# The last layer's gate and value columns: two of four 512-column pairs as seven block products, with weight sums made in earlier layers

## The chip, the cores and the metric

The kernel runs on one core of one Trainium2 chip. The metric is the device time of one execution in microseconds (us), the median over runs. The engines are TensorE (PE, with its weight loads PEld), VectorE (DVE), ScalarE (ACT), GpSimd (POOL), and SyncE (SP), which here only issues DMAs.

## What is computed

A decoder trunk of four residual layers on x of 256 tokens by 1024 channels, all in float32. Each layer normalises x by its rms (h) and adds a mixer's output. Layers 0 and 3 are of kind A, layer 1 is dilated attention (B), layer 2 is pooling (C). Only kind A is changed:

```python
def mixer_a(h, w_in, v_gain, w_s, b_s, w_out):
    proj = h @ w_in
    u = proj[..., :A_WIDTH]                                   # A_WIDTH = 2048
    v = rms_norm(proj[..., A_WIDTH:2 * A_WIDTH], v_gain)
    z = proj[..., 2 * A_WIDTH:]
    ...
    mixed = jnp.einsum('gij,bcjgd->bcigd', ws, v) + b_s.T[None, None, :, :, None]
    y = u * mixed * jax.nn.silu(z)
    return y @ w_out
```

So h (256 x 1024) is multiplied by three blocks of 2048 columns, v, z and u; v is mixed over tokens by lower-triangular matrices of 128 x 128 (two per 512 columns), and u, mixed v and silu(z) are multiplied and projected back.

## The kernel before

**Float32 products in three passes.** Every operand of a matmul is split into a high part (ACT, `hi_of`, L82) and a low part, the rest (DVE, `lo_of`, L85). `mm3` (L75 to L79) makes one product of three matmuls: high by high, high by low, low by high.

**Weights as a stream.** All weights lie in DRAM in the order of use, as 272 units of 128 x 1024 (512 KB). `load_units` (L131) issues each from SP into one of 4 raw buffers `wr`; a raw buffer is free when DVE has made the low part of the unit that lay there. `split_hi` and `split_units` (L141, L151) make `w..h` and `w..l` into 7 buffers, some 5 units ahead of use. PE uses a unit in 12 matmuls of 128x512 (two row blocks, two token halves, three passes). In layer 3 the units are: v 208 to 223, then for each n of 0 to 3 z and u with four units each (z0 224 to 227, u0 228 to 231, z1 232 and on), and 256 to 271 for the output projection.

**Order of the work.** The program is written out by one Python thread. Projections are loops that call `step` (L167) after each row block; it calls `tick` (L102), which advances a counter and lets tasks that are due write out their next instructions. A task is a generator that yields the number of ticks until its next piece. So the code's order, and with it each engine's queue, comes from these delays; each engine then works through its queue in that order.

**Kind A.** `layer_a` (L489) makes v for n of 0 to 3 (`v_task`, L501: square sums on ACT, times gain on DVE, split), then for each n projects z, applies silu on ACT (L593), projects u; `mix_task` (L544) makes the token mix into PSUM and `y_task` (L558) multiplies on DVE (L566, L569), transposes y on PE (L577) through the one PSUM bank `tr`, and splits it (`y..h`, `y..l`). PSUM has four banks `pp` for projections, one `tr`, three `at`. In kind A layers (`gated`, L208) x isn't normalised before it is transposed: the rms factor r of a token is applied later, in silu, in the squares of v, in u (L566), and in the mixing matrices (POOL, L527). Layers 1 and 2 scale x first into a tile `xs` (`norm_scale`, L240).

**Attention (layer 1).** For each pair of heads hp and group g a projection gives q and k; `qk_task` (L635) normalises them (ACT L654), rotates (DVE L663 to L668), transposes token half 0 on PE (L675) into `tr`, splits it (ACT L677, DVE `low`, L683, written to `qk..l`), then does the same with half 1, in the same bank.

## Time and profile before

| | us |
|---|---|
| median of 3 runs | 837.23 |
| lowest and highest run | 836.3, 837.82 |
| the profiled execution | 837.29 |
| its span, first to last instruction | 835.6 |
| PE busy | 829.3 (99%) |
| DVE busy | 543.9 (65%) |
| ACT busy | 491.6 (59%) |
| mean DMA rate over the span | 179 GB/s |

A row of the timeline is: start, duration, engine and line, operation, written tile <- read tiles, shapes, count; in brackets the idle time of that engine just ahead and what ended it. A row of a group ends in: busy us in all, mean ns of one | idle time ahead, and its releaser. The granted clock of PE was 1.000. Matmuls are pipelined: one of 128x512 is shown as 0.39 us long, but the next starts earlier, and the spacing of starts is what counts. A window row has: window, length, busy us (instructions) of PE, PEld, DVE, ACT and POOL, the granted clock, DMA share and GB/s.

### The profile page before, as it was taken

How to read it: one execution, taken by the hardware profiler on the slowest of the kernel's cores; microseconds unless marked ns; L12 is line 12 of the kernel's file. 1: busy time of each engine (PE TensorE's matmuls, PEld its weight loads, DVE VectorE, ACT ScalarE, POOL GpSimd, SP SyncE). 2: the span in 40 equal slices, each digit the busy share in tenths (PEclk: the TensorE clock that was granted, in tenths of full speed). 3: DMA queues.
4: the chain of work that ended last, by engine and by line, in shares of the span. 5: the costliest groups of instructions: out<-in, count | busy, mean ns of one | idle time of the engine just before them, and what ended most of it. 6: DMA issues, size and time to landing. Idle time of an engine off the chain costs nothing.

```text
span 835.6 us, 12346 instructions
## 1 busy us (share of the span) xinstructions
PE 829.3 (99%) x4589; PEld 718.1 (86%) x4589; DVE 543.9 (65%) x906; ACT 491.6 (59%) x913; POOL 43.6 (5%) x71
## 2 busy tenths in 40 slices
PE   8999999999999999999999999999999999999998
PEld 7888888888988888888888889999988888888886
DVE  4876656646757577577577575898754777556551
ACT  6765444436758687787787576455544666434340
POOL 1201000000000010010010021000000000000000
PEclk9999999999999999999999999999999999999999
DMA  7876565562745345345355278447564466454541
GB/s 285 281 239 220 177 201 180 175 200 83 256 165 178 109 158 187 111 161 183 110 164 181 62 225 279 161 136 257 197 225 152 141 233 209 157 184 160 176 151 51
DMA packets 42028, 149.58 MB, mean 179 GB/s; under 512 B 4880, under 2 KB 5408, under 8 KB 41840
## 3 DMA queue, kind: packets, MB, share of 16 engines
q1 hardware_dynamic: 40704, 144.72, 52.1%
q0 software_dynamic: 976, 3.79, 1.3%
q8 instruction: 36, 0.59, 0.3%
q10 hardware_dynamic: 288, 0.28, 0.1%
q14 instruction: 24, 0.20, 0.1%
HBM read 147.72 MB, written 1.05 MB: 178 GB/s over the span
## 4 chain that ended last, share of the span: by engine, by line
PE 99%; DMA 1%; SPq 0%; DVE 0%; issue 0%
PE wo L77 6%; PE wo L79 6%; PE wo L78 6%; PE qk L77 5%; PE qk L79 5%; PE qk L78 5%; PE v L77 5%; PE v L79 5%; PE v L78 5%; PE z L79 4%; PE z L77 3%; PE z L78 3%; PE u L77 3%; PE u L78 3%; PE u L79 3%; PE cz L77 2%
## 5 line engine op out<-in xcount | busy, mean ns | idle before, releaser
L650 POOL TENSOR_TENSOR qr<-qm,m 128x8 f32<-128x8 f32 x12 | 19.7, 1638 | 227.9 <-DVE qm L649 227.9
L645 ACT ACTIVATE junk<-qk 128x128 bf16<-128x128 f32 x96 | 26.7, 278 | 7.3 <-PE qk L79 4.7
L566 DVE SCALAR_TENSOR_TENSOR sz<-u,m,sz 128x512 f32<-128x512 f32 x16 | 11.9, 746 | 27.3 <-PE u L79 27.3
L654 ACT ACTIVATE qn<-qk,qr 128x128 f32<-128x128 f32 x96 | 27.6, 382 | 3.4 <-POOL qr L650 3.4
L459 DVE TENSOR_TENSOR x<-wo,x 128x512 f32<-128x512 f32 x16 | 11.0, 690 | 20.1 <-PE wo L79 20.0
L255 ACT ACTIVATE hT<-hp,gT 128x128 fp32r<-128x128 f32 x48 | 13.1, 383 | 14.9 <-PE hp L251 14.9
L649 DVE TENSOR_SCALAR qm<-qs 128x8 f32<-128x8 f32 x12 | 2.1, 172 | 26.8 <-ACT junk L645 26.8
L260 DVE SCALAR_TENSOR_TENSOR hT<-hp,gT,hT 128x128 fp32r<-128x128 f32 x48 | 13.5, 343 | 8.8 <-ACT hT L255 8.8
L593 ACT ACTIVATE sz<-z,m 128x512 f32<-128x512 f32 x16 | 10.7, 687 | 13.9 <-PE z L79 13.9
L645 ACT ACTIVATION_READ_ACCUMULATOR junk<-qk 128x1 f32 x96 | 18.8, 196 | 0.0
L506 ACT ACTIVATE junk<-v,m 128x512 bf16<-128x512 f32 x16 | 11.0, 686 | 11.6 <-PE v L79 11.4
L507 DVE TENSOR_TENSOR vv<-v,kc 128x512 f32<-128x512 f32 x16 | 10.7, 687 | 8.8 <-ACT junk L506 8.4
L229 ACT ACTIVATE junk<-x 128x512 bf16<-128x512 f32 x16 | 10.2, 640 | 9.6 <-DVE x L459 9.4
L744 ACT ACTIVATE p<-p,rl 128x384 f32<-128x384 f32 (+1 forms) x16 | 11.5, 769 | 4.8 <-DVE rl L743 4.8
L569 DVE SCALAR_TENSOR_TENSOR yy<-mx,bs,sz 128x256 f32<-128x256 f32 x32 | 14.0, 479 | 0.6
L675 PE MATMUL qt<-ident,qn 128*128 128x128 f32 x96 | 14.4, 272 | 0.0
L667 DVE TENSOR_TENSOR rb<-qn,kcb 128x32 f32<-128x32 f32 x96 | 13.8, 185 | 0.0
L675 PEld LDWEIGHTS qt<-ident,qn 128*128 128x128 f32 x96 | 11.7, 140 | 2.3
L237 POOL TENSOR_TENSOR r<-ms,m 128x1 f32<-128x1 f32 x4 | 3.1, 785 | 175.3 <-DVE ms L234 175.3
L740 ACT ACTIVATE p<-p,nb 128x768 f32<-128x768 f32 x8 | 7.5, 937 | 7.6 <-DVE nb L739 7.6
L663 DVE TENSOR_TENSOR ra<-qn,kcb 128x64 f32<-128x64 f32 x48 | 10.6, 221 | 1.0 <-ACT qn L654 0.4
L775 PE MATMUL pt<-ident,p 128*128 128x128 f32 x48 | 9.9, 274 | 0.0
(2771 smaller groups left out, 3254.4 us busy)
## 6 DMA issues: line engine op xcount, KB each, us to landing
wr<-in_wts_dram SPq DMA_DIRECT2D x271, 512.0 KB, 3.9
kc<-in_a_wsT_dram POOLq DMA_DIRECT2D x2, 512.0 KB, 7.5
kc<-in_a_v_gain_dram POOLq DMA_DIRECT2D x1, 1024.0 KB, 5.1
out_dram<-x SPq DMA_DIRECT2D x4, 256.0 KB, 2.0
kc<-in_a_v_gain_dram POOLq DMA_DIRECT2D x1, 768.0 KB, 6.6
kcb<-in_masks_dram POOLq DMA_DIRECT2D x1, 576.0 KB, 8.2
x<-in_x_dram SPq DMA_DIRECT2D x2, 256.0 KB, 4.2
x<-in_x_dram SPq DMA_DIRECT2D x1, 512.0 KB, 6.6
```

The costliest lines, as they stand in the source:

```text
L77: nc.tensor.matmul(out_ap, lh[0], rh[0], start=start, stop=False, skip_group_check=True)
L78: nc.tensor.matmul(out_ap, lh[0], rh[1], start=False, stop=False, skip_group_check=True)
L79: nc.tensor.matmul(out_ap, lh[1], rh[0], start=False, stop=stop, skip_group_check=True)
L255: nc.scalar.activation(h_parts(layer)[0][:, k, t * P:(t + 1) * P], pt[:, k % 4], AF.Copy, scale=gT[:, layer, k:k + 1])
L260: nc.vector.scalar_tensor_tensor(hTl, pt[:, k % 4], gT[:, layer, k:k + 1], hTh.bitcast(F32), op0=ALU.mult, op1=ALU.subtract)
L566: nc.vector.scalar_tensor_tensor(us[t], up[t], r_tok[t][:, 0:1], us[t], op0=ALU.mult, op1=ALU.mult)
L569: nc.vector.scalar_tensor_tensor(y[:, sl], mxs[n][t][:, sl], bsT[:, 2 * n + gg:2 * n + gg + 1], us[t][:, sl], op0=ALU.add, op1=ALU.mult)
L645: nc.scalar.activation(junk[:, :HD], ov[t][:, h], AF.Square, accum_out=ssq[t][:, h:h + 1])
L650: nc.gpsimd.tensor_tensor(rqs, ms, m05_row[:, :8], op=ALU.pow)
L654: nc.scalar.activation(qn[t][:, h], ov[t][:, h], AF.Copy, scale=rq[t][:, h:h + 1])
L667: nc.vector.tensor_tensor(rb[:, hs, s0:s0 + 16], qn[t][:, hs, s1:s1 + 16], c, op=ALU.mult)
L675: nc.tensor.transpose(pts[t][:, h], qn[t][:, h], ident)
```

## The change

For n = 1 and n = 3 of layer 3 (`SEVEN`) the pair z, u is made by a scheme of seven block products. h is taken as two token halves by two channel halves, the weights of z and u as two channel halves by two column blocks (z and u): a 2 x 2 by 2 x 2 block product, in eight block products before. With sums of blocks of h and of weights on the one side, and additions of results on the other, seven suffice. A block product is 12 matmuls of 128x512 and uses two units of weights in six matmuls each.

- `sums_of_quarters`: four of the seven products need sums of weight blocks. They are made in 16 parts, each of four quarters of 128 x 256 that are loaded into one tile (`qs`, the buffer of `xs`; 512 KB), added by four DVE operations in place, and stored to DRAM (`sums`). Load, 6 ticks, additions, 3 ticks, store, 4 ticks, next load. Five parts begin in layer 0 after v, eleven in layer 1 after the first qk projection.
- The weight stream of a changed pair has 14 units: eight from `sums` and six of the units as before (the other two are read for the sums alone). Units after it are counted on, so that the stream has 284.
- `sums_task` makes the sums of blocks of h during v's third and fourth projection of layer 3: eight additions of 128x512 on DVE, and four splits.
- Since sums of token halves can't carry one factor r per token, layer 3 now scales x first, as layers 1 and 2 do (`late` instead of `gated`).
- `seven_products` accumulates into four `pp` banks: zb (two products), xb (three), yb and wb. ACT copies intermediate sums out: q5 from zb, p1, n2 and n3 from xb, where a later product adds to the same bank. DVE combines them (`first_task`, `second_task`) ahead of `y_task`.

Cut from the diff: the DRAM pool, a bound (`n_seq` in `split_units`), and the places in `v_task` where r is left out when not `late`.

```diff
 LAST_LAG = 1
 LAST_AHEAD = 3
 WARM = 13
+SEVEN = (1, 3)
+FIRST_PARTS = 5
 @with_exitstack
...
     loaded = [0]
     split = [0]
+    seq = list(range(n_units))
+    sums = {(n, j): dp.tile([4, P, UNIT], F32, name=f"sums{n}{j}") for n in SEVEN for j in range(2)}
+    def seven_units(n):
+        return n_units - 48 + 8 * n
+    for n in reversed(SEVEN):
+        z = seven_units(n)
+        seq[z:z + 8] = [e[j] for e in (((n, 0, 0), (n, 0, 1)), (z, z + 1), (z + 6, z + 7), ((n, 3, 0), (n, 3, 1)),
+                                       (z + 2, z + 3), ((n, 2, 0), (n, 2, 1)), ((n, 1, 0), (n, 1, 1)))
+                        for j in range(2)]
+    n_seq = len(seq)
     def load_units(n):
-        while loaded[0] < min(n, n_units):
-            u = loaded[0]
-            raw = wp.tile([P, 2, HALF], F32, tag="wr", name=f"wr{u}", bufs=RAW_BUFS)
-            nc.sync.dma_start(raw, wts[u].rearrange("p (k n) -> p k n", n=HALF))
+        while loaded[0] < min(n, n_seq):
+            i = loaded[0]
+            raw = wp.tile([P, 2, HALF], F32, tag="wr", name=f"wr{i}", bufs=RAW_BUFS)
+            src = sums[seq[i][0], seq[i][2]][seq[i][1]] if isinstance(seq[i], tuple) else wts[seq[i]]
+            nc.sync.dma_start(raw, src.rearrange("p (k n) -> p k n", n=HALF))
             raws.append(raw)
             loaded[0] += 1
+    def sums_of_quarters(parts):
+        for n, j, c in parts:
+            z = seven_units(n) + j
+            cs = slice(c * 256, (c + 1) * 256)
+            q = cp.tile([P, 4, 256], F32, tag="xs", name=f"qs{n}{j}{c}", bufs=1)
+            nc.sync.dma_start(q, wts[z:z + 8:2][:, :, cs].rearrange("i p c -> p i c"))
+            yield 6
+            for a, b in ((0, 2), (2, 3), (3, 0), (1, 3)):
+                nc.vector.tensor_tensor(q[:, a], q[:, a], q[:, b], op=ALU.add)
+            yield 3
+            nc.sync.dma_start(sums[n, j][:, :, cs].rearrange("i p c -> p i c"), q)
+            yield 4
     lowered = [0]
     def split_hi(n):
-        while split[0] < min(n, n_units):
+        while split[0] < min(n, n_seq):
             u = split[0]
             load_units(u + 1)
             hi, lo = pair(wp, [P, 2, HALF], "w", f"w{u}", W_BUFS)
...
         split_units(u + 1)
         return units[u]
-    def step(i, ahead=AHEAD):
-        tick()
+    def step(i, ahead=AHEAD, due=True):
+        if due:
+            tick()
         if i % 2 == 0:
             split_hi(used[0] + ahead)
         else:
...
     nc.gpsimd.memset(m05_row[:, :8], -0.5)
     r_rows = [m05_row[:, 8 * t + 8:8 * t + 9] for t in range(2)]
-    def gated(layer):
-        return layer in (0, DEPTH - 1)
+    def late(layer):
+        return layer == 0
     r_tok = [None, None]
     def h_parts(layer):
-        o = 16 if gated(layer) else 0
+        o = 16 if layer in (0, DEPTH - 1) else 0
         return [hT[:, o + i * KT * S:o + (i + 1) * KT * S].rearrange("p (k s) -> p k s", s=S) for i in range(2)]
     hcur = [None, None]
...
     def norm_rms(layer, t, ss):
         ms = tiny(1, f"ms{layer}{t}")
         nc.vector.scalar_tensor_tensor(ms, ss[:, 0:1], EPS, ss[:, 1:2], op0=ALU.add, op1=ALU.add)
-        r = r_rows[t] if gated(layer) else tiny(1, f"r{layer}{t}")
+        r = r_rows[t] if late(layer) else tiny(1, f"r{layer}{t}")
         r_tok[t] = r
         nc.gpsimd.tensor_tensor(r, ms, m05[:, 0:1], op=ALU.pow)
         return r
     def norm_scale(layer, t, r):
-        if gated(layer):
+        if late(layer):
             return xt[t].rearrange("p (n c) -> p n c", c=HALF)
         xs = cp.tile([P, 2, HALF], F32, tag="xs", name=f"xs{layer}{t}", bufs=1)
         for n in range(2):
...
             ys = []
             for t in range(2):
                 y = tmp("yy", f"yy{layer}{n}{t}", 2)
-                nc.vector.scalar_tensor_tensor(us[t], up[t], r_tok[t][:, 0:1], us[t], op0=ALU.mult, op1=ALU.mult)
+                if late(layer):
+                    nc.vector.scalar_tensor_tensor(us[t], up[t], r_tok[t][:, 0:1], us[t], op0=ALU.mult, op1=ALU.mult)
+                else:
+                    nc.vector.tensor_tensor(us[t], up[t], us[t], op=ALU.mult)
                 for gg in range(2):
                     sl = slice(gg * 256, (gg + 1) * 256)
                     nc.vector.scalar_tensor_tensor(y[:, sl], mxs[n][t][:, sl], bsT[:, 2 * n + gg:2 * n + gg + 1],
...
                     yield 1
             done.add(("y", layer, n))
+        if layer == DEPTH - 1:
+            smh, sml = pair(pl, [P, 4, 4, P], "sm", f"sm{layer}", 1)
+        def sums_task():
+            q = {}
+            for k, t in ((1, 1), (0, 1), (0, 0), (1, 0)):
+                d = q[k, t] = tmp("sz", f"sq{layer}{k}{t}", 4).rearrange("p (k c) -> p k c", c=P)
+                hh, hl = (a[:, 4 * k:4 * k + 4, t * P:(t + 1) * P].bitcast(F32) for a in hcur)
+                nc.vector.tensor_tensor(d, hh, hl, op=ALU.add)
+                yield 1
+            a11, a12, a21, a22 = q[0, 0], q[1, 0], q[0, 1], q[1, 1]
+            for i, (d, a, b, op) in enumerate(((a22, a21, a22, ALU.subtract), (a21, a11, a21, ALU.subtract),
+                                               (a11, a22, a11, ALU.subtract), (a12, a12, a11, ALU.add))):
+                nc.vector.tensor_tensor(d, a, b, op=op)
+                hi_of(smh[:, i], d)
+                yield 1
+                lo_of(sml[:, i], d, smh[:, i])
+                yield 1
+            done.add(("sums", layer))
+        S_A21_A22, S_A11_A21, S_REST, S_A12_REST = range(4)
+        def seven_products(n):
+            need(("sums", layer))
+            def sm(i):
+                return lambda k: (smh[:, i, k], sml[:, i, k])
+            def product(o, a, first):
+                for j in range(2):
+                    w = next_unit()
+                    for kk in range(2):
+                        k = 2 * j + kk
+                        mm3(o, a(k), (w[0][:, kk], w[1][:, kk]), first and k == 0, k == 3)
+                        step(kk, due=kk == 1)
+            def minus(o, name):
+                d = tmp("vv", name, 2)
+                nc.scalar.activation(d, o, AF.Copy, scale=-1.0)
+                return d
+            def keep(o, name):
+                d = tmp("sz", name, 4)
+                nc.scalar.activation(d, o, AF.Copy)
+                return d
+            r = {}
+            def keep_task(key, how, o):
+                r[key] = how(o, f"{key}{layer}{n}")
+                yield 1
+            zb = pp(f"zb{layer}{n}")
+            product(zb, sm(S_A21_A22), True)
+            spawn(keep_task("q5", keep, zb), 1)
+            xb = pp(f"xb{layer}{n}")
+            product(xb, lambda k: h_t(k, 0), True)
+            spawn(keep_task("p1", keep, xb), 1)
+            product(zb, sm(S_A12_REST), False)
+            product(xb, sm(S_REST), False)
+            spawn(keep_task("n2", minus, xb), 1)
+            yb = pp(f"yb{layer}{n}")
+            product(yb, lambda k: h_t(4 + k, 0), True)
+            z0, u0 = r["p1"], r["n2"]
+            def first_task():
+                nc.vector.tensor_tensor(z0, yb, z0, op=ALU.add)
+                nc.scalar.activation(z0, z0, AF.Silu)
+                yield 1
+                nc.vector.tensor_tensor(u0, zb, u0, op=ALU.add)
+            spawn(first_task(), 1)
+            spawn(mix_task(n), 2)
+            product(xb, sm(S_A11_A21), False)
+            spawn(keep_task("n3", minus, xb), 1)
+            wb = pp(f"wb{layer}{n}")
+            product(wb, lambda k: h_t(4 + k, 1), True)
+            z1, u1 = r["n3"], r["q5"]
+            def second_task():
+                nc.vector.tensor_tensor(u1, u1, z1, op=ALU.add)
+                nc.vector.tensor_tensor(z1, wb, z1, op=ALU.subtract)
+                nc.scalar.activation(z1, z1, AF.Silu)
+                yield 1
+            spawn(second_task(), 1)
+            spawn(y_task(n, (u0, u1), (z0, z1)), 2)
         for n in range(4):
             spawn(v_task(n, first if first and n == 0 else
                          proj_tok(f"v{layer}{n}", skew=layer if n == 0 else None)))
+            if layer == DEPTH - 1 and n == 0:
+                spawn(sums_task(), 4)
+        if layer == 0:
+            spawn(sums_of_quarters(parts[:FIRST_PARTS]))
         for n in range(4):
+            if layer == DEPTH - 1 and n in SEVEN:
+                seven_products(n)
+                continue
             zp = proj_tok(f"z{layer}{n}")
             us = []
             for t in range(2):
                 sz = tmp("sz", f"sz{layer}{n}{t}", 4)
-                nc.scalar.activation(sz, zp[t], AF.Silu, scale=r_tok[t][:, 0:1])
+                nc.scalar.activation(sz, zp[t], AF.Silu, scale=r_tok[t][:, 0:1] if late(layer) else 1.0)
                 us.append(sz)
             spawn(mix_task(n), 4)
             spawn(y_task(n, proj_tok(f"u{layer}{n}"), us))
...
             for g in range(NG):
                 spawn(qk_task(hp, g, proj_tok(f"qk{hp}{g}", skew=layer if hp == 0 and g == 0 else None)))
                 if hp == 0 and g == 0:
+                    spawn(sums_of_quarters(parts[FIRST_PARTS:]))
                     gate(0)
                     gate(1)
             o = proj_tok(f"v01{hp}")
...
     box = {}
+    parts = [(n, j, c) for n in SEVEN for j in range(2) for c in range(4)]
     def after_ws():
         spawn(load_b())
```

On DVE in layer 1, the second half's rotation of qk10, the split of unit 101, and the low part of qk10's first half (`qk10l`); `ra`, `rb`, `qn` are the rotation's tiles. Before:

```order
L663 TENSOR_TENSOR ra101_2839<-qn101_2749,kcb_634 128x64
L667 TENSOR_TENSOR rb101_2840<-qn101_2749,kcb_634 128x2x16 x2
L668 TENSOR_TENSOR qn101_2749<-ra101_2839,rb101_2840 128x4x32
L85 TENSOR_TENSOR w101l_2849<-wr101_2688,w101h_2848 128x1024
L683 SCALAR_TENSOR_TENSOR qk10l_2745<-qt100_2866,gv_638,qk10h_2744 128x2x128 x2
L85 TENSOR_TENSOR w102l_2874<-wr102_2742,w102h_2873 128x1024
```

and now, with the additions of one part (`qs301`: n = 3, j = 0, c = 1, of each the index in `parts`):

```order
L803 TENSOR_TENSOR ra101_2910<-qn101_2820,kcb_646 128x64
L807 TENSOR_TENSOR rb101_2911<-qn101_2820,kcb_646 128x2x16 x2
L808 TENSOR_TENSOR qn101_2820<-ra101_2910,rb101_2911 128x4x32
L170 TENSOR_TENSOR qs301_2792<-qs301_2792 128x256 x4
L88 TENSOR_TENSOR w101l_2920<-wr101_2757,w101h_2919 128x1024
L823 SCALAR_TENSOR_TENSOR qk10l_2816<-qt100_2941,gv_650,qk10h_2815 128x2x128 x2
L88 TENSOR_TENSOR w102l_2949<-wr102_2813,w102h_2948 128x1024
```

The block of four additions stands between the rotation and the split of w101, so `qk10l` stands behind it.

On DVE in layer 0, between the y products of n = 0 (`yy001`) and its low parts `y00l`; the second of the 16 parts, in the changed kernel:

```order
L612 SCALAR_TENSOR_TENSOR yy001_765<-mx001_711,bs0_254,sz001_666 128x256 x2
L88 TENSOR_TENSOR w29l_778<-wr29_687,w29h_777 128x1024
L170 TENSOR_TENSOR qs101_727<-qs101_727 128x256 x4
L88 TENSOR_TENSOR y00l_760<-yp000_786,y00h_759 128x4x128
L88 TENSOR_TENSOR w30l_807<-wr30_719,w30h_806 128x1024
L88 TENSOR_TENSOR y00l_760<-yp001_815,y00h_759 128x4x128
```

Before, the row of `qs101` is not there, and `y00l` follows w29l.

On ACT in layer 3, the highs of the weights and the first pair changed (n = 1). Before, with the two silu (`sz31`) and the highs of y (`y31h`):

```order
L593 ACTIVATE sz310_7484<-z31_0_7396,m05_66 128x512
L593 ACTIVATE sz311_7486<-z31_1_7397,m05_66 128x512
L82 ACTIVATE w241h_7496<-wr241_7420 128x1024
L82 ACTIVATE w242h_7514<-wr242_7445 128x1024
L82 ACTIVATE w243h_7546<-wr243_7464 128x1024
L82 ACTIVATE w244h_7564<-wr244_7482 128x1024
L82 ACTIVATE w245h_7594<-wr245_7506 128x1024
L82 ACTIVATE y31h_7576<-yp310_7603 128x4x128
```

and now, from the copy of p1 on:

```order
L673 ACTIVATE p131_7615<-xb31_7571 128x512
L85 ACTIVATE w242h_7623<-wr242_7569 128x1024
L85 ACTIVATE w243h_7635<-wr243_7585 128x1024
L85 ACTIVATE w244h_7647<-wr244_7603 128x1024
L85 ACTIVATE w245h_7660<-wr245_7618 128x1024
L668 ACTIVATE n231_7666<-xb31_7571 128x512
L85 ACTIVATE w246h_7674<-wr246_7630 128x1024
L85 ACTIVATE w247h_7686<-wr247_7642 128x1024
L697 ACTIVATE p131_7615<-p131_7615 128x512
```

The copy n2 of the accumulator xb stands behind the highs of four units, w242 to w245; PE's third product into xb stands behind n2.

More of the change, by code (lines that the diff above doesn't have):

```diff
@@ L505, in v_task @@
             for t in range(2):
[L506 removed]
+                nc.scalar.activation(junk, o[t], AF.Square, scale=r_tok[t][:, 0:1] if late(layer) else 1.0,
+                                     accum_out=vs[t][:, n:n + 1])
                 nc.vector.tensor_tensor(vv[t], o[t], kc[:, n * HALF:(n + 1) * HALF], op=ALU.mult)
```

12 lines of the change are left out of this document (7 added, 5 removed).

## The prediction

> **What bounds the kernel now.** I read the page's busy times and its chain first, then what TensorE (PE) waited for.
>
> ```profile
> PE 829.3 (99%) x4589; PEld 718.1 (86%) x4589; DVE 543.9 (65%) x906; ACT 491.6 (59%) x913; POOL 43.6 (5%) x71
> PE 99%; DMA 1%; SPq 0%; DVE 0%; issue 0%
> PE warm L223 <- POOL m L205: 1.4, 1, 1.4
> PE hp L327 <- DMA x<-in_x_dram: 0.7, 2, 0.4
> ```
>
> PE works for 829.3 of 835.6 us, and its only waits (2.1 us) lie at the start. So every matmul that goes is a gain of its full spacing, and every new wait of PE is a loss of its full length: nothing downstream can give it back. DVE is idle for a third of the time, but off PE's path only as long as PE's inputs and PSUM banks are ready when PE comes. The question is what 16 blocks of additions, put into DVE's queue at fixed places, and a denser stretch in layer 3 do to these margins.
>
> **What it removes.** Per changed pair, 96 matmuls of 128x512 become 84, twice: 24 go. Their spacing stands in PE's timeline in layer 3; from the first matmul of w243 to the first of w245 there are two units, 24 matmuls:
>
> ```profile
> 747.65 0.39 PE L77 MATMUL z<-w243h,hT 128*128 128x512 f32 x1
> 753.09 0.39 PE L77 MATMUL u<-w245h,hT 128*128 128x512 f32 x1
> ```
>
> 753.09 - 747.65 = 5.44 us. That is the whole gain: **-5.44**.
>
> **The sums of quarters.** Each of the 16 parts is four additions of 128x256 in a chain, the later ones reading what an earlier one wrote. Nearest rows:
>
> ```profile
> L798 DVE TENSOR_TENSOR szT<-o,szT 128x256 f32<-128x256 f32 x8 | 3.4, 422 | 4.2 <-PE o L79 4.1
> L569 DVE SCALAR_TENSOR_TENSOR yy<-mx,bs,sz 128x256 f32<-128x256 f32 x32 | 14.0, 479 | 0.6
> 299.79 0.28 DVE L667 TENSOR_TENSOR rb<-qn,kcb 128x32 f32<-128x32 f32 x2
> 300.11 0.29 DVE L668 TENSOR_TENSOR qn<-ra,rb 128x128 f32<-128x128 f32 x1
> 300.32 1.22 DVE L85 TENSOR_TENSOR w101l<-wr,w101h 128x1024 fp32r<-128x1024 f32 x1
> 301.76 0.88 DVE L683 SCALAR_TENSOR_TENSOR qk10l<-qt,gv,qk10h 128x256 fp32r<-128x256 f32 x2 [0.22 <-ACT qk10h L677]
> 303.44 0.60 PE L675 MATMUL qt<-ident,qn 128*128 128x128 f32 x4
> 303.79 0.48 PE L77 MATMUL qk<-w98h,hT 128*128 128x512 f32 x1
> ```
>
> An independent operation starts about 0.08 before the last one ends (300.11 + 0.29 against 300.32), one that needs the last result 0.04 after its end (rb's end 300.07, qn 300.11). A part thus holds DVE for 4 x 0.422 + 3 x 0.04 - 0.08 = 1.73, taken as 1.75 us; at 0.479 each and 0.1 between them it is 2.2, and without the waits (3 x 0.34 + 0.42 - 0.08) 1.36. I take 1.75, since the chain is there in the code. The Trainium skill, page "VectorE: DVE Perf Modes", section "The DRAIN you can't avoid", says that the next operation does not start before the pipe is empty and that a semaphore between two costs nothing extra. By that the chain costs what unchained additions do, the 1.36; the rows above speak against it, an overlap of 0.08 without a dependence and a gap of 0.04 with one.
>
> Where does such a block delay PE? In layer 1, PE's second group of transposes (qt) takes the one "tr" bank over from DVE's low(0), and low(0) ends just ahead: 301.76 + 0.88 = 302.64, PE at 303.44, room 0.80. The order of the changed kernel puts a block two rows ahead of low(0) there. Idle time of DVE on the way absorbs some (0.22): 1.75 - 0.22 - 0.80 = 0.73 us of wait. The same reading at the other places where a block stands ahead of a low(0) or, in layer 0, of y00l:
>
> ```profile
> 80.42 0.69 DVE L85 TENSOR_TENSOR y00l<-yp,y00h 128x512 fp32r<-128x512 f32 x1
> 82.35 0.60 PE L577 MATMUL yp<-ident,yy 128*128 128x128 f32 x4
> 215.89 1.23 DVE L85 TENSOR_TENSOR w75l<-wr,w75h 128x1024 fp32r<-128x1024 f32 x1 [0.18 <-ACT w75h L82]
> 217.30 0.87 DVE L683 SCALAR_TENSOR_TENSOR qk00l<-qt,gv,qk00h 128x256 fp32r<-128x256 f32 x2 [0.19 <-ACT qk00h L677]
> 218.98 0.60 PE L675 MATMUL qt<-ident,qn 128*128 128x128 f32 x4
> 321.76 1.23 DVE L85 TENSOR_TENSOR w108l<-wr,w108h 128x1024 fp32r<-128x1024 f32 x1 [0.19 <-ACT w108h L82]
> 325.53 0.88 DVE L683 SCALAR_TENSOR_TENSOR qk12l<-qt,gv,qk12h 128x256 fp32r<-128x256 f32 x2 [0.40 <-ACT qk12h L677]
> 327.26 0.49 PE L675 MATMUL qt<-ident,qn 128*128 128x128 f32 x3
> 388.06 0.88 DVE L683 SCALAR_TENSOR_TENSOR qk22l<-qt,gv,qk22h 128x256 fp32r<-128x256 f32 x2 [0.40 <-ACT qk22h L677]
> 389.79 0.60 PE L675 MATMUL qt<-ident,qn 128*128 128x128 f32 x4
> 434.98 1.23 DVE L85 TENSOR_TENSOR w140l<-wr,w140h 128x1024 fp32r<-128x1024 f32 x1 [0.19 <-ACT w140h L82]
> 438.74 0.88 DVE L683 SCALAR_TENSOR_TENSOR qk31l<-qt,gv,qk31h 128x256 fp32r<-128x256 f32 x2 [0.39 <-ACT qk31h L677]
> 440.43 0.60 PE L675 MATMUL qt<-ident,qn 128*128 128x128 f32 x4
> ```
>
> y00l: room 82.35 - 81.11 = 1.24, wait 0.51. qk00l: idle 0.37, room 0.81, wait 0.57. qk12l: 0.59 and 0.85, 0.31. qk22l: 0.40 and 0.85, 0.50. qk31l: 0.58 and 0.81, 0.36. With qk10l the six make **+2.98**. At 1.36 a part they make 0.8; at 2.2 a part 5.7. The other ten blocks stand ahead of weight splits alone, or of a group's second low, which nothing soon waits for; a split unit is used many us after it is made (w245l below ends at 742.41, its first matmul starts at 753.09), so I cost them at nothing. Without that lead they would be 1.75 each, 17.5 in all.
>
> The loads and stores of the parts (16 x 2 x 512 KB) go through SP, between the weight loads. A store waits there for its additions, and the next part's load waits for that store to land, both with weight loads behind them. The worst place is layer 0, where loads land late:
>
> ```profile
> wr<-in_wts_dram SPq DMA_DIRECT2D x7, 512.0 KB, 6.4
> kcb<-in_masks_dram POOLq DMA_DIRECT2D x1, 576.0 KB, 8.2
> wr<-in_wts_dram SPq DMA_DIRECT2D x271, 512.0 KB, 3.9
> ```
>
> The first two are from the window of 60 to 80 us, the last from the whole span (last column: us from issue to landing). From the store of the first part to the additions of the second there are ten ticks, each of six matmuls (1.36 us): 13.6. A store and a load at 6.4 each take 12.8 and are in time, so I take 0; at 8.2 each they take 16.4, and the additions, right ahead of y00l, come 2.8 late. That is the upper bound.
>
> **Layer 3's norm** is now scaled ahead of the transposes (4 more 128x512 operations on DVE). The same form already runs into layers 1 and 2, and its 32 transposes had 0.1 us of idle time in all:
>
> ```profile
> L251 PE MATMUL hp<-ident,xs 128*128 128x128 f32 x32 | 4.2, 273 | 0.1
> ```
>
> So **+0.1**, at most 0.5 for one late r. The eight additions, four highs and four lows for the sums of h lie under the v products, where DVE is idle for 30% (14.02 of 20 us busy); they are 8 x 0.69 there, spread over two projections, and nothing waits for them before the first changed pair:
>
> ```profile
> 700.00:720.00 20.00, 20.00 (x97) 16.80 (x96) 14.02 (x17) 9.52 (x11) 0.00 (x0) 1.00 0.54 180
> ```
>
> **The stretch of seven products.** A unit of weights is now used by six matmuls, 5.44 / 4 = 1.36 us, so a product of two units takes 2.72. The stretch has 14 units where the pair had 8. And the accumulators zb and xb are used again, so PE must wait until ACT has copied them out. Take before's stretch with T0 = 738.52 as a template:
>
> ```profile
> 736.00 1.06 ACT L82 ACTIVATE w245h<-wr 128x1024 fp32r<-128x1024 f32 x1 [3.12 <-PE u L79]
> 738.52 0.39 PE L77 MATMUL z<-w240h,hT 128*128 128x512 f32 x1
> 741.19 1.21 DVE L85 TENSOR_TENSOR w245l<-wr,w245h 128x1024 fp32r<-128x1024 f32 x1
> 742.52 0.69 DVE L85 TENSOR_TENSOR y31l<-yp,y31h 128x512 fp32r<-128x512 f32 x1
> L593 ACT ACTIVATE sz<-z,m 128x512 f32<-128x512 f32 x16 | 10.7, 687 | 13.9 <-PE z L79 13.9
> wr<-in_wts_dram SPq DMA_DIRECT2D x10, 512.0 KB, 3.3
> ```
>
> The last row is the window from 736 to 770. DVE leaves the last pair's y work at T0 + 2.67. Then by the order come five lows (1.22 less the overlap of 0.08, so 1.14 each) and two y lows up to w241l: 2.67 + 5 x 1.14 + 2 x 0.69 = 9.75, about 9.9 with one wait for ACT. Only then is w245 loaded (four raw buffers); landing 3.3 to 3.9 later gives 13.2 to 13.8; its high takes 1.06, and behind it on ACT stands n2, the copy of xb, 0.69: done at 14.9 to 15.6. PE wants xb for the sixth product after five products and two groups of transposes, 5 x 2.72 + 2 x 0.45 = 14.5 (a group of four shifts the matmuls by 0.35, 303.44 to 303.79, and 0.1 after it, an estimate from the 0.48 of the next one). Wait 0.4 to 1.1, taken as 0.8; the earlier copy p1 comes out 0.1 late at most by the same count (w241 lands at T0 + 7.1, copy done 8.85, wanted 9.06), taken as 0.1. Two stretches: **+1.8**, bounds 0.2 and 3.0 (a slow landing). Weights themselves are not late: nine units are split or loaded at T0.
>
> **Sum.** -5.44 + 2.98 + 0.1 + 1.8 = -0.56. The profiled execution took 837.29 (span 835.6 and 1.7 outside), the median of the runs is 837.23, so 837.29 - 0.56 = **836.7 us**. About 0.2% (1.7 us) is what a measurement of this kernel can tell from no change, so the likeliest answer is "the gain is eaten". With the bounds of the terms (0.8 to 5.7, 0.2 to 3.0) this case runs from 834.5 to 839.
>
> **Rivals.** *The covers hold* (0.25): the additions run closer to 1.36, DVE catches up, n2 is in time. Then -5.44 + 0.8 + 0.2 = -4.4, 832.9; with the middle term for n2, 834.5. For it: DVE is idle 35% of the time. Against: rooms of 0.8 are smaller than any block.
>
> *Slower: the raw buffers pace the stretch* (0.10). One unit passes four raw buffers in (landing + 1.06 + 1.22) / 4; at a landing of 3.9 that is 1.54, just PE's mean of 21.5 / 14, at 6.4 (the row of 60 to 80 us) 2.17. w241, the first not staged at T0, would be split at 3.9 + 6.4 + 2.3 = 12.6, in time for 13.1, but each of the next four falls 0.64 back: 2.1 us late by w245, 4.2 over both stretches, so 836.7 + 4.2 = 840.9. It decides from a landing of 5.4 on. For it: 14 units (7.34 MB) in 21.5 us are 341 GB/s, and the busiest stretches now reach 356. Against: landings in layer 3 are now near 3.3 to 3.9.
>
> ```profile
> 762.71 0.39 PE L77 MATMUL z<-w248h,hT 128*128 128x512 f32 x1
> 758.00:760.00 2.00, 2.00 (x11) 1.64 (x10) 0.33 (x1) 0.00 (x0) 0.00 (x0) 1.00 0.96 356
> ```
>
> (21.5 is the pair of before, 762.71 - 738.52 = 24.2, less 12 matmuls.) The Trainium skill, page "DMA: Bandwidth & Descriptors", section "Specifications", gives about 358 GB/s as what HBM lets one core have; the row agrees. By that limit the 14 units take 20.5 us, an estimate, so the rate alone would not make them late, only with other traffic beside it.
>
> *Slower: dearer additions* (0.08): 2.2 a part gives 5.7 in place of 2.98, 839.4; at about 1.85 (six waits 0.1 longer) nothing is left of the gain, and the loss grows from there.
>
> *Not what it says* is excluded by the order: 84 matmuls stand there for 96.
>
> **Chances.** Forecast 0.57, most of it within 1.7 of 837.2. Faster by over 0.2% (under 835.6): 0.25 and some 0.10 of the forecast, 0.35. Slower (over 838.9): 0.10 + 0.08, 0.18. Same: 0.47. The range takes in the dearer additions and most of the first rival, and leaves out the raw buffers and the first rival's best end: 833.0 to 839.6.
>
> **What would show it.** In the profile after: PE waits for DVE qk..l at five places in layer 1 and for y00l in layer 0, 0.3 to 0.7 each, 3 us in all; PE waits for ACT n2 ahead of xb's third use, 0.8 twice; four qs additions in about 1.8 us; no PE wait on w..l. Wrong: no waits on low(0) (the first rival), or waits on w..l or wr in layer 3 (the second).

## The result, and the profile after

The changed kernel took 843.58 us (median of 4 runs, 843.26 to 846.08), the kernel before 836.82 beside it (836.3 to 837.82): ratio 1.0086, interval 1.0064 to 1.0108. It is 6.8 us slower, where 0.5 less was forecast and 839.6 was the range's upper end.

The page of the profile after, its busy times and its chain:

```profile
PE 827.1 (98%) x4565; PEld 713.0 (85%) x4565; DVE 593.8 (71%) x1006; ACT 508.5 (60%) x937; POOL 42.0 (5%) x69
PE 83%; DVE 7%; DMA 5%; ACT 3%; issue 2%; POOL 0%; DVEq 0%; SPq 0%; ACTq 0%
```

The chain was PE for 99%; now 17% of it is something else. What PE waited for (us in all, times, longest):

```profile
PE xb L80 <- ACT n L668: 2.5, 2, 1.5
PE yp L620 <- DVE y00l L88: 2.5, 1, 2.5
PE yp L620 <- DVE y31l L88: 1.1, 1, 1.1
PE qt L815 <- DVE qk10l L823: 0.6, 1, 0.6
PE qt L815 <- DVE qk00l L823: 0.3, 1, 0.3
PE qt L815 <- DVE qk22l L823: 0.3, 1, 0.3
PE yp L620 <- DVE y33l L88: 0.3, 1, 0.3
PE wo L80 <- DVE n L711: 0.3, 1, 0.3
```

Of the five waits that the prediction named in layer 1, three are in this list; the other two are too short for it, but show in the starts of the units (below). n's and y00l's are there and larger, and y31l, y33l and the last bank (wo) were not named. To see how much each stage lost, I read the start of the first matmul of some units from PE's timeline in each run and took differences:

| from the first matmul of | before | after | more |
|---|---|---|---|
| unit 24 to unit 28 (layer 0, z and u of n = 1) | 11.85 | 16.34 | +4.49 |
| unit 64 to unit 150 (layer 1 up to its output projection) | 286.63 | 289.44 | +2.81 |
| first changed pair (n = 1) | 24.18 | 22.73 | -1.45 |
| pair n = 2 | 24.19 | 25.51 | +1.32 |
| second changed pair (n = 3) | 24.19 | 23.31 | -0.88 |
| output projection of layer 3, to the last matmul | 44.26 | 45.45 | +1.19 |

The stages not in the table differ by 0.1 at most, except the first 20 us, where PE's slow start varies from run to run (unit 4 begins at 18.8 to 21.0). A changed pair should be 24.19 - 2.72 = 21.47. So layer 3, from the first changed pair to the last matmul, takes 117.00 in place of 116.82: its whole gain of 5.44 is given back inside the layer. What makes the kernel slower are the 7.3 us of layers 0 and 1.

**Layer 0.** DVE's rows around y00l, then PE's, then what SP issued:

```profile
79.82 1.21 DVE L88 TENSOR_TENSOR w29l<-wr,w29h 128x1024 fp32r<-128x1024 f32 x1
81.63 1.81 DVE L170 TENSOR_TENSOR qs<-qs 128x256 f32<-128x256 f32 x4 [0.60 <-DMA qs<-in_wts_dram]
83.35 0.68 DVE L88 TENSOR_TENSOR y00l<-yp,y00h 128x512 fp32r<-128x512 f32 x1
```

```profile
81.19 0.39 PE L82 MATMUL z<-w25h,hT 128*128 128x512 f32 x1
84.09 1.11 PE L620 MATMUL yp<-ident,yy 128*128 128x128 f32 x4 [2.51 <-DVE y00l L88]
84.86 0.78 PE L80 MATMUL z<-w26h,hT 128*128 128x512 f32 x1
85.43 0.63 PE L81 MATMUL z<-w26l,hT 128*128 128x512 f32 x1
85.86 0.63 PE L82 MATMUL z<-w26h,hT 128*128 128x512 f32 x1
86.29 0.63 PE L80 MATMUL z<-w26h,hT 128*128 128x512 f32 x1
```

```profile
66.66 0.43 SPq L172 DMA_DIRECT2D sums<-qs  x1
75.66 0.38 SPq L167 DMA_DIRECT2D qs<-in_wts_dram  x1
```

The first part's store goes out at 66.66 and takes 9.0 us, and the second part's load has to wait for it: it goes out at 75.66 and lands 5.9 later, at 81.6. The additions wait 0.60 for it, take 1.81, and y00l and PE's transposes stand behind them. But the late load is the smallest of three parts. DVE itself comes late to this place, because the high of w28 waits longer for its weights. Before, then after:

```profile
73.82 1.06 ACT L82 ACTIVATE w28h<-wr 128x1024 fp32r<-128x1024 f32 x1 [4.56 <-DMA wr<-in_wts_dram]
74.44 1.06 ACT L85 ACTIVATE w28h<-wr 128x1024 fp32r<-128x1024 f32 x1 [6.19 <-DMA wr<-in_wts_dram]
```

Unit 24's first matmul starts at 76.43 before and at 75.29 after, so w28h comes 1.76 us later as PE counts, and w28l and DVE's y work behind it 1.75. That, the 0.60 and the 1.72 of the additions make y00l 4.07 late; the room of 1.24 comes off, and PE starts its transposes 2.88 later than before, counted from unit 24 (the 2.51 in the row is idle time, from the drawn end of the matmul ahead). The run l3_ahead (below) has the same code in layer 0, and there the quarters land in time, with no idle time ahead of the additions; PE still waits 1.8:

```profile
82.31 1.80 DVE L170 TENSOR_TENSOR qs<-qs 128x256 f32<-128x256 f32 x4
84.03 0.68 DVE L88 TENSOR_TENSOR y00l<-yp,y00h 128x512 fp32r<-128x512 f32 x1
84.77 0.66 PE L620 MATMUL yp<-ident,yy 128*128 128x128 f32 x4 [1.82 <-DVE y00l L88]
```

What delays w28 is the first part. Its additions (60.99, 1.80 us) stand ahead of w23l and w24l, whose raw buffers w27 and w28 take next; both lows come 1.7 later, and so do the two loads, into a stretch where the first part's store moves as well. Without the additions (no_adds) w28h is in time again, with the same loads and stores. How much of its delay is the later issue and how much the shared DMA was not taken apart.

Then something follows that the prediction didn't have: the matmuls after the wait start 0.43 apart in place of 0.227. The windows answer (PE busy, then the other engines, then the granted clock):

```profile
84.00:88.00 4.00, 3.91 (x13) 3.30 (x14) 3.04 (x5) 2.49 (x3) 0.00 (x0) 0.57 0.49 115
```

The granted clock was 0.57 in these 4 us. From the transposes to unit 28 PE takes 7.54 in place of 5.92, so the slow clock costs 1.6 us. Wait and slow clock, 2.9 and 1.6, together make the 4.49.

**Layer 3, first changed pair.** ACT's rows at n2 and PE's at the sixth product, and DVE's and PE's at the transposes of the pair's y:

```profile
734.65 1.06 ACT L85 ACTIVATE w245h<-wr 128x1024 fp32r<-128x1024 f32 x1 [0.17 <-DMA wr<-sums]
735.62 0.58 ACT L668 ACTIVATE n<-xb 128x512 f32<-128x512 f32 x1
736.25 0.50 PE L80 MATMUL xb<-w242h,sm3h 128*128 128x512 f32 x1 [0.97 <-ACT n L668]
752.46 0.68 DVE L88 TENSOR_TENSOR y31l<-yp,y31h 128x512 fp32r<-128x512 f32 x1
753.20 0.66 PE L620 MATMUL yp<-ident,yy 128*128 128x128 f32 x4 [1.10 <-DVE y31l L88]
```

The stretch begins at 720.55, so n2 is done at T0 + 15.65, just above the forecast's upper 15.6. What ACT waited for in that stretch:

```profile
ACT w247h L85 <- DMA wr<-in_wts_dram: 1.6, 1, 1.6
ACT w243h L85 <- DMA wr<-sums: 0.9, 1, 0.9
ACT w242h L85 <- DMA wr<-sums: 0.9, 1, 0.9
ACT w246h L85 <- DMA wr<-in_wts_dram: 0.6, 1, 0.6
```

From w242 on, each high waits for its load to land, and DVE's lows wait for the highs. So DVE, idle for 3.7 us in the middle of the stretch, comes to the pair's last sums and its y work late.

### The profile page after: what moved, and what is told of

Same layout as the page of the kernel before. It is cut to its first block, busy times and chain, and to the rows that moved or that the text cites. A ratio compares the mean times of both kernels' runs of the same rounds, so it can differ in the third digit from the quotient of the medians.

```text
span 841.7 us, 12513 instructions
## 1 busy us (share of the span) xinstructions
PE 827.1 (98%) x4565; PEld 713.0 (85%) x4565; DVE 593.8 (71%) x1006; ACT 508.5 (60%) x937; POOL 42.0 (5%) x69
## 4 chain that ended last, share of the span: by engine, by line
PE 83%; DVE 7%; DMA 5%; ACT 3%; issue 2%; POOL 0%; DVEq 0%; SPq 0%; ACTq 0%
PE wo L80 6%; PE wo L82 6%; PE wo L81 6%; PE v L82 5%; PE v L80 5%; PE v L81 5%; PE qk L82 4%; PE qk L80 4%; PE qk L81 4%; PE u L81 2%; PE u L80 2%; PE u L82 2%; PE cz L81 2%; PE cz L80 2%; PE cz L82 2%
## 5 line engine op out<-in xcount | busy, mean ns | idle before, releaser
L170 DVE TENSOR_TENSOR qs<-qs 128x256 f32<-128x256 f32 x64 | 27.1, 424 | 2.5 <-DMA qs<-in_wts_dram 0.9
L815 PE MATMUL qt<-ident,qn 128*128 128x128 f32 x96 | 14.5, 273 | 1.4 <-DVE qk10l L823 0.6
L620 PE MATMUL yp<-ident,yy 128*128 128x128 f32 x64 | 10.3, 285 | 4.0 <-DVE y00l L88 2.5
L620 PEld LDWEIGHTS yp<-ident,yy 128*128 128x128 f32 x64 | 7.9, 144 | 7.2 <-DVE y00l L88 2.9
L607 DVE SCALAR_TENSOR_TENSOR sz<-u,m,sz 128x512 f32<-128x512 f32 x8 | 6.0, 746 | 10.1 <-PE u L82 10.1
L612 DVE SCALAR_TENSOR_TENSOR yy<-mx,bs,sz 128x256 f32<-128x256 f32 x24 | 10.5, 480 | 0.4
```

Of the source, the lines that this page charges most:

```text
L170: nc.vector.tensor_tensor(q[:, a], q[:, a], q[:, b], op=ALU.add)
L620: nc.tensor.transpose(pt[:, k], ys[t][:, k * P:(k + 1) * P], ident)
L815: nc.tensor.transpose(pts[t][:, h], qn[t][:, h], ident)
```

## The experiments

A is the time from the first matmul of unit 4 to that of unit 232 (the first changed pair), B from there to the last matmul, both from the starts in PE's timeline of the profiled run; they leave out PE's start. The ratio is to the kernel before, timed in the same rounds (its median was 836.28 to 837.79 in them).

| run | median us | ratio, interval | A | B |
|---|---|---|---|---|
| before | 836.82 | | 693.95 | 116.82 |
| after | 843.58 | 1.0086 (1.0064 to 1.0108) | 701.29 | 117.00 |
| no_adds | 837.66 | 1.0005 (0.9996 to 1.0015) | 694.01 | 117.15 |
| no_sums | 836.99 | 0.9999 (0.9989 to 1.0010) | 693.95 | 118.57 |
| part1_later | 843.35 | 1.0065 (1.0042 to 1.0088) | 698.35 | 117.82 |
| split_adds | 840.45 | 1.0035 (1.0022 to 1.0048) | 696.43 | 117.93 |
| pool_adds | 841.82 | 1.0051 (1.0036 to 1.0067) | 697.33 | 118.03 |
| hid_adds | 851.99 | 1.0191 (1.0170 to 1.0213) | 708.87 | 117.77 |
| safe_adds | 838.10 | 1.0011 (1.0002 to 1.0021) | 694.87 | 118.64 |
| n2_early | 844.66 | 1.0081 (1.0060 to 1.0103) | 699.37 | 117.36 |
| l3_order | 846.04 | 1.0103 (1.0082 to 1.0123) | 700.49 | 118.87 |
| l3_ahead | 845.66 | 1.0099 (1.0075 to 1.0122) | 699.15 | 119.74 |
| hid_pool | 854.16 | 1.0214 (1.0198 to 1.0230) | 706.52 | 120.06 |
| hid_raw5 | 846.83 | 1.0117 (1.0081 to 1.0154) | 710.68 | 111.97 |
| hid_all | 850.34 | 1.0169 (1.0153 to 1.0185) | 709.38 | 116.81 |
| after_raw5 | 837.61 | 1.0005 (0.9996 to 1.0015) | 699.45 | 112.84 |
| safe_raw5 | 832.91 | 0.9948 (0.9934 to 0.9963) | 694.94 | 113.06 |
| before_raw5 | 837.57 | 1.0000 (0.9990 to 1.0009) | 693.99 | 116.81 |

Eight runs (after, no_adds, no_sums, part1_later, split_adds, pool_adds, hid_adds, safe_adds) have the same order of work in layer 3, and their B goes from 117.00 to 118.64. Five (after, n2_early, l3_order, l3_ahead, after_raw5) have the same layers 0 and 1, and their A goes from 699.15 to 701.29. What differs by less than that from profile to profile shows no effect.

The theory at first: DVE's additions at their places in the queue cost PE the time in layers 0 and 1, and in layer 3 queue places again (n2, the y work). The rivals: the DMA traffic, or the weights' loads, set the pace.

### Layers 0 and 1: the additions

**no_adds and no_sums.** First without the additions, then with nothing at all done ahead of layer 3:

```diff
-            for a, b in ((0, 2), (2, 3), (3, 0), (1, 3)):
-                nc.vector.tensor_tensor(q[:, a], q[:, a], q[:, b], op=ALU.add)
```

```diff
-            spawn(sums_of_quarters(parts[:FIRST_PARTS]))
-                    spawn(sums_of_quarters(parts[FIRST_PARTS:]))
-            src = sums[seq[i][0], seq[i][2]][seq[i][1]] if isinstance(seq[i], tuple) else wts[seq[i]]
+            src = wts[seven_units(seq[i][0]) + 2 * seq[i][1] + seq[i][2]] if isinstance(seq[i], tuple) else wts[seq[i]]
```

> The parts are still loaded and stored through DRAM, but the four DVE additions of each part are left out (the stored blocks are raw quarters, so four of the seven products use wrong weights). Theory (the additions' places in DVE's queue cost PE the time): PE no longer waits for y00l in layer 0 (2.5 us, and the 1.25 us of slow clock behind it) nor for qk..l in layer 1 (about 2.2 us), so about 843.5 - 6.0 = 837.5 us, with the waits on n2 and y31l in layer 3 as in the changed kernel. Rival (the added DMA traffic of 16.8 MB in layers 0 and 1 is what costs): the time stays near 842 to 843.5.

> Nothing is done for the sums in layers 0 and 1: no loads, additions or stores; the seven products read 14 plain units of weights (so four products use wrong weights). Theory (queue places): the same time as with the additions alone left out, 837.5 us, within 0.5; n2 still waits 1.1 and 1.7 us. Rival (DMA traffic): 1 us or more below the run without additions.

A is 694.01 and 693.95, as before: without the additions the loads and stores cost layers 0 and 1 nothing. The rival (DMA traffic) falls for these layers. PE's longest waits without the additions are those of layer 3 and one at the start (warm):

```profile
PE xb L80 <- ACT n L666: 2.7, 2, 1.6
PE warm L258 <- POOL m L240: 1.4, 1, 1.4
PE yp L618 <- DVE y31l L88: 1.2, 1, 1.2
```

Both runs also bound what mending the additions alone can give, with layer 3 as it is: no gain at all over the kernel before.

**part1_later.** Only the second part's additions are moved:

```diff
-            yield 6
+            late_part = (n, j, c) == (1, 0, 1)
+            yield 9 if late_part else 6
...
-            yield 4
+            yield 1 if late_part else 4
```

> Only the second part's additions move 3 ticks later (its next load comes 3 ticks closer), behind both y00l in layer 0. Theory (a late load ahead of y00l, and the slow clock after the wait): 2.7 us of wait and 1.25 us of slow clock go, 843.5 - 3.9 = 839.6 us. Rival (a block of four additions costs PE wherever it stands in this layer): 842 us or more.

The time did not show it (843.35). The stages do in part: units 24 to 28 took 12.25 in place of 16.34, but units 28 to 40 took 37.54 for 36.55, since the next part's load now followed its store too closely and the wait came back there. B is 0.8 longer, within its spread, and PE's start was slower (clock 0.61 between 8 and 12 us). So the second part is confirmed as what turns DVE's delay into y00l's wait, not the size of the gain. The edit takes the additions and their late load away from y00l together and doesn't tell them apart; l3_ahead above does.

**split_adds and pool_adds.** Two pairs in place of a block of four, and the additions on POOL:

```diff
+            for i, (a, b) in enumerate(((0, 2), (2, 3), (3, 0), (1, 3))):
                 nc.vector.tensor_tensor(q[:, a], q[:, a], q[:, b], op=ALU.add)
+                if i == 1:
+                    yield 1
-            yield 3
+            yield 2
```

```diff
-                nc.vector.tensor_tensor(q[:, a], q[:, a], q[:, b], op=ALU.add)
+                nc.gpsimd.tensor_tensor(q[:, a], q[:, a], q[:, b], op=ALU.add)
```

> The four additions of a part are written as two pairs, one tick apart, at the same places else. Theory (a block of 1.8 us is longer than the idle time and the room ahead of low(0)): a pair holds DVE for about 0.9, under the 1.0 to 1.2 of idle time and room, so PE's waits for qk..l in layer 1 go and with them 2.2 to 2.8 us; y00l in layer 0 still waits for the late load, less by 0.9: 843.5 - 3.4 = 840.1 us. Rival (any addition ahead of low(0) costs, since DVE is full there): the second pair delays the second low instead, and the time stays within 1 us of 843.5.

> The additions are made by POOL, which is 5% busy, in the place of DVE. Theory (it is DVE's queue that costs PE): the waits of PE in layers 0 and 1 go as in the run without additions, 838 us, unless POOL's own work for the q and k norms (1.6 us each) comes late behind a block. Rival (POOL and DVE slow each other, or the norms come late): 841 us or more.

The pairs gave 840.45, as expected, but for another reason in part: layer 1 (unit 64 to 150) is at 288.58, only 0.9 less, because at qk10l both pairs still stand ahead of low(0). Layer 0 gained most: its wait for y00l fell to 0.3, with no slow clock after it. On POOL an addition took 1.02 us on average (the median of the 64 is 0.74), and PE waited 0.6 to 0.7 for low(0) at four places: layer 1 is at 289.96, longer than with DVE. The rival that was on record, POOL and DVE slowing each other, shows in the same operation of DVE's rotation, first in the kernel before, then beside POOL's additions (213.74 to 217.98 us):

```profile
214.62 0.22 DVE L663 TENSOR_TENSOR ra<-qn,kcb 128x64 f32<-128x64 f32 x1
215.68 0.76 DVE L803 TENSOR_TENSOR ra<-qn,kcb 128x64 f32<-128x64 f32 x1
```

The wait for y00l is gone there too.

**hid_adds.** The additions ahead of qm in layer 1 and ahead of the product with u in layer 0 (the same four additions, written by `add_part`):

```diff
             def rms():
+                if (hp, g) != (0, 0):
+                    pump(part["k"] < 16, 1)
...
+            if layer == 0 and n:
+                pump(True, 3)
```

> The whole change, with the additions put where DVE is idle: in layer 1 right ahead of qm, where DVE waits some 2.2 us for ACT's squares, in layer 0 ahead of the products with u, where it waits 3.9 us for PE. Theory (the places, not the work, cost PE the time in layers 0 and 1): the time of the run without additions, 837.5 us, within 0.7, with layers 0 and 1 as long as in the kernel before. Rival (1.8 us of DVE work per part cost wherever they stand): 839.5 us or more.

851.99: the worst of these, and a miss. What DVE waited for says why:

```profile
DVE qs L173 <- DMA qs<-in_wts_dram: 23.0, 8, 4.2
```

Projections follow each other every 8 ticks, too soon for a store and a load one behind the other, so DVE stood 23 us in front of additions with everything else behind it. Idle time is no cover where the work's own data come late. Whether the work could be hidden stayed open until the next run.

**safe_adds.** The order of the change, with each part's additions held back while a low(0), or a y product, is on its way to PE (`critical`), so that the loads keep their lead (in layer 0 the first wait is 7 ticks in place of 6):

```diff
-            yield 6
+            yield lag
+            while critical[0]:
+                yield 1
...
             assert rms_due[0] is None
+            critical[0] += 1
...
             low(0)
+            critical[0] -= 1
```

> The change with its additions held back while a low(0) in layer 1, or a y product, waits to be handed to PE; each load is issued 4 ticks behind the store ahead of it, as in the change, so that none is late. Theory (place in the queue and late loads, not the work): layers 0 and 1 as long as in the kernel before within 0.7 us, and 837.5 us in all, since layer 3 alone gives back its gain. Rival (1.8 us of DVE work per part cost PE wherever they stand): 839.5 us or more, with waits at other places of layer 1.

A is 694.87, 0.9 above before, and the time 838.10. Of the 0.9, 0.39 lies right ahead of unit 92, where PE waits for ACT's p, and 0.37 between units 92 and 93, where attention's product waits for the low part pT00l. w28h is in time here: the first part's additions now stand behind w23l. The work of 27 us of additions is nearly free; its places and its loads made the loss.

### Layer 3: why the gain was given back

**n2_early, l3_order, l3_ahead.** Three steps of moving work forward in the queues: n2 right behind its product; n3, the last sums and the y work as well; and the weight splits 4 and 3 units ahead in the last two products:

```diff
-            spawn(keep_task("n2", minus, xb), 1)
+            spawn(keep_task("n2", minus, xb))
```

```diff
-            spawn(keep_task("n3", minus, xb), 1)
+            spawn(keep_task("n3", minus, xb))
-            spawn(second_task(), 1)
-            spawn(y_task(n, (u0, u1), (z0, z1)), 2)
+            spawn(second_task())
+            spawn(y_task(n, (u0, u1), (z0, z1)), 1)
```

```diff
-            product(xb, sm(S_A11_A21), False)
+            product(xb, sm(S_A11_A21), False, 4)
-            product(wb, lambda k: h_t(4 + k, 1), True)
+            product(wb, lambda k: h_t(4 + k, 1), True, 3)
```

> The copy n2 is put into ACT's queue right behind the fourth product, ahead of the high of the next unit. Theory (n2 stands behind a high that waits for its load): PE's waits for n before the sixth product (1.1 and 1.7 us) go, 843.5 - 2.8 = 840.7 us. Rival (the weights' loads set the pace of the stretch, the copy only shows it): the wait moves to a weight split, 842.5 us or more.

> In the stretches of layer 3 n2 and n3 are copied right behind their products, and the last sums and the y work are written one tick earlier. Theory (DVE's y work of the changed pair comes late because it stands behind weight lows): the wait for n2 goes (2.8 us) and part of the waits for y31l, y33l and the last bank (3.5 us with the ones that replaced n2's in the run with n2 early): between 838.5 and 840.5 us. Rival (DVE has more work in the stretch than PE, whatever the order): as in the run with n2 early, the gain is given back in the next pair, 841.5 us or more.

> As the run with the earlier order, and the weight splits run 4 and 3 units ahead in place of 5 in the last two products of a stretch, so that two lows fewer stand ahead of the y work. Theory (lows ahead of the y work): another 1 to 2 us less than that run, since the weights have 3 us to spare. Rival (DVE's total work): no gain, PE waits for a low instead.

The changed pairs came down to between 21.5 and 21.9 us, nearly the full gain, in all three; but the pair n = 2 went from 25.51 to 27.02, 28.54 and 26.57, the output projection (45.45 in the change) to 46.9 to 49.5, and B did not fall (117.36, 118.87, 119.74). The wait was moved, not removed. With n2 early PE waits for:

```profile
PE wo L80 <- DVE n L711: 1.8, 1, 1.8
PE yp L620 <- DVE y31l L88: 1.2, 1, 1.2
PE yp L620 <- DVE yy L612: 1.1, 1, 1.1
```

So queue places as the cause of layer 3's loss, my theory, fell: whoever is served first, someone behind waits.

**hid_raw5 and hid_pool.** On the kernel with the additions ahead of qm: a fifth raw buffer in layer 3, or four lows of each stretch on POOL. That tells late loads from too much work on DVE:

```diff
+            if extra and i >= EXTRA and (i - EXTRA) % 5 == 0:
+                raw = extra[0].tile([P, 2, HALF], F32, tag="wrx", name=f"wr{i}", bufs=1)
...
-            load_units(u + 1 + RAW_BUFS)
+            load_units(u + 1 + RAW_BUFS + (u + 1 + RAW_BUFS >= EXTRA))
```

```diff
+POOL_LOWS = (239, 242, 245, 248, 261, 264, 267, 270)
...
+            if u in POOL_LOWS:
+                nc.gpsimd.tensor_tensor(units[u][1], raws[u], units[u][0].bitcast(F32), op=ALU.subtract)
```

> As the run with the hidden additions, and a fifth raw buffer in layer 3. Theory A (with four raw buffers loads are issued too late in the stretches, so highs, and n2 behind them, come late): the wait for n2 (2.8 us) goes and part of those for y31l and y33l, 834.5 us. Theory B (DVE has more work in layer 3's second half than fits beside PE's shortened time): the wait moves, 836.5 us or more.

> As the run with the hidden additions, and eight weight lows of layer 3 (four per stretch) are made by POOL in the place of DVE; a 128x256 addition took POOL 0.74 us, so each some 3 us there. Theory B (DVE's work): the waits for y31l, y33l and the last bank go (2.5 us or more), 835 us. Theory A (late loads): n2's wait stays and little is gained, 836.5 us or more.

> Hidden additions, the fifth raw buffer, the eight lows on POOL and n2 right behind its product. If A and B both hold, most of the waits of layer 3 go: 832.5 to 834 us, below the kernel before. If PE's time isn't what bounds layer 3, 836 us or more.

Layers 0 and 1 are those of hid_adds, so only B counts (A is 706.52 to 710.68 in the four profiles). The fifth buffer: 111.97, 5.8 us less than hid_adds, and 4.85 less than the kernel before, nearly the whole 5.44. DVE's work is the same there. The lows on POOL: 120.06, worse. All of it together: 116.81, so what the buffer gives is taken back by POOL's lows or by n2's new place. The pair n = 2 takes 27.27 in hid_all, as in n2_early (27.02), and 24.97 in hid_pool, where n2 isn't moved. That points to n2's place; no run took the two apart. Theory A holds. Theory B finds no support: with DVE's work unchanged, the buffer alone brought nearly the whole gain. The lows on POOL are no clean test of it, since POOL's additions lengthened DVE's own rows in pool_adds.

**after_raw5, safe_raw5, before_raw5.** The buffer alone on the changed kernel, with the held-back additions, and on the kernel before:

> The changed kernel with nothing else than the fifth raw buffer in layer 3. Theory (late loads cost layer 3 its gain): the waits for n2, y31l and y33l go and the time falls by 4.5 to 5 us, to 838.5 to 839 us. Rival (the run with the hidden additions had gained it by their delays): less than 2.5 us.

> The same with the fifth raw buffer in layer 3. By the theory both losses go: 836.5 - 4.9 = 831.5 to 832.5 us, below the kernel before. Rival: 834.5 us or more.

> The kernel before with the fifth raw buffer in layer 3 and nothing else. Theory (late loads cost something only where a pair has 14 units in 21.5 us): no change, within 0.1% of the kernel before. Rival (the fifth buffer helps layer 3 as such): 1 us or more below it.

The buffer alone: B 112.84, 4.2 less than in the change, and the time from 843.58 to 837.61. Not all of that is the buffer's: A is 1.8 shorter too, since the slow clock behind y00l is missing in that profile. PE's longest waits in that run, without those of the start:

```profile
PE yp L626 <- DVE y00l L88: 1.8, 1, 1.8
PE qt L821 <- DVE qk10l L829: 0.6, 1, 0.6
PE xb L80 <- ACT n L674: 0.5, 1, 0.5
PE qt L821 <- DVE qk22l L829: 0.4, 1, 0.4
PE yp L626 <- DVE y33l L88: 0.3, 1, 0.3
```

n is down from 2.5 to 0.5 and y31l is gone; the waits of layers 0 and 1 are still there. The second changed pair takes 21.47, the first still 22.27. Without the change the buffer does nothing (ratio 1.0000). With both causes taken away, safe_raw5 runs in 832.91, ratio 0.9948 (0.9934 to 0.9963): faster than both kernels, by 0.5% of the one before. PE's waits there, beside the start's:

```profile
PE xb L80 <- ACT n L680: 0.4, 1, 0.4
PE yp L631 <- DVE y33l L88: 0.3, 1, 0.3
```

## Why the prediction was wrong, point by point

- **The gain of 5.44** was right: with waits away, a changed pair takes 21.47 (after_raw5, second pair), 2.72 less than 24.19. The norm of layer 3, forecast at 0.1, cost nothing: units 208 to 232 take 67.67 in both kernels.
- **A part's 1.75** was right: 1.81 as the trace shows it, less the overlap. 64 additions took 27.1 us, 424 ns each, with a gap of 0.04 between them (4 x 0.424 + 3 x 0.04 = 1.82), more than the 1.36 that was worked out without waits. So the measurement speaks against the rule of the Trainium skill weighed there (page "VectorE: DVE Perf Modes", section "The DRAIN you can't avoid"), that a semaphore between two operations costs nothing extra.
- **The five waits in layer 1**: 2.47 forecast, 2.39 measured by the starts of the units behind them: 0.53 for qk00l (0.57 forecast), 0.75 for qk10l (0.73), 0.29 for qk12l (0.31), 0.53 for qk22l (0.50), 0.29 for qk31l (0.36). Right in place and size. The rest of the 2.81 is mostly a sixth place that wasn't forecast: 0.36 between units 92 and 93, where attention's product waits for pT00l.
- **y00l**: 0.51 forecast, the block's 1.75 less a room of 1.24, with a late load of the second part taken as 0 (at most 2.8). This step failed: PE came 2.88 late. The room was read where DVE is in time, and the first part's block was one of the ten costed at nothing, because "a split unit is used many us after it is made". That is so, but a split also frees a raw buffer: the loads behind it went out later, and w28 brought DVE 1.75 late to the y work, more than the whole room. The late load added 0.60. The store took 9.0 us and the load 5.9, where 6.4 each were put in; the row that warned of it was quoted (kcb's 8.2 in that window).
- **The slow clock** (1.6 us here) was not in the sum at all. It comes and goes: of the five profiles with these layers 0 and 1, two show it behind y00l, with 16.34 (after) and 15.59 (l3_order) from unit 24 to unit 28; the others take 14.24 to 14.37, and the kernel before 11.85.
- **n2** was forecast at 0.8 twice, 0.4 to 1.1; it was 1.1 and 1.7 (735.62 + 0.58 against T0 + 14.5). Its mechanism was right: behind a high that waits for its load. The load of w245 goes out at T0 + 9.55, where 9.9 was forecast. The landing was mis-sized: 3.3 to 3.9, from a stretch with 8 units; w245's high starts 4.55 after its load goes out, with ACT waiting for it. The medians of the changed kernel's whole run are later too (3.9 before):

```profile
wr<-in_wts_dram SPq DMA_DIRECT2D x267, 512.0 KB, 4.4
wr<-sums SPq DMA_DIRECT2D x16, 512.0 KB, 4.7
```

- **"Weights themselves are not late"** was true and misled. PE waited for a weight only at the start, but ACT and DVE did in the stretch, and what stands behind the weights in their queues, the copies of the accumulators and the y work, came late. Beside n2 it cost 1.3 us in pair n = 2 and 1.2 in the output projection (y31l, y33l and the last bank), 2.5 us that the sum didn't have. The rival "the raw buffers pace the stretch" (0.10) was the mechanism; I looked for its price only at PE's use of the weights, and put its threshold at a landing of 5.4. Four buffers bind at 4.4 to 4.7 already, because of what waits behind; with five, the second pair of after_raw5 runs at its full speed, though its loads from `in_wts_dram` take 5.4.
- **The range** was narrower than its own terms. Their upper bounds add up to 840.7 (-5.44 + 5.7 + 0.1 + 3.0), and with the late load's 2.8 to 843.5, not to the 839 that the text gives. And 356 GB/s is not the busiest that the kernel before reaches: 690 to 692 us shows 373, and 10 to 12 us 415, so these traces show no limit at 356.

## What to carry to other kernels

A denser stretch made loads slower here as well as more frequent: take the landing from the densest stretch of the trace, and ask what stands in the queues behind the engine that waits for them, not only whether its product comes in time. When reordering only moves a wait to the next consumer, look for the bound upstream; here it was a buffer. Work ahead of a weight split isn't free because the split is used late: the split also frees the buffer that the next load waits for. Work put into idle time needs its own data early: a store and a load one behind the other were longer here than the gaps between.
